# An encoder block on one core: eight attention steps moved into an earlier projection unit, and their operands into a free weight buffer

## The chip, the core and the metric

The kernel runs on one core of a Trainium2 chip. A core has a matrix engine (TensorE, PE in the profile, with its weight loads as PEld), a vector engine (VectorE, DVE), an activation engine (ScalarE, ACT), a general engine (GpSimd, POOL) and a queue that issues transfers (SyncE, SP). Each engine works through its own list of instructions in order, and a semaphore makes one wait for another. Matmuls write into PSUM, which is used here as eight banks of 128 x 2 KB; a bank can take a new result only once the last reader of the old one is through.

The metric is the device time of one execution in microseconds (us): the median of 3 runs of the kernel before is 972.11 us (970.75 to 972.4).

## The reference, cut to what matters

One encoder layer over two sequences with 16 meta tokens each; the 18 blocks of 128 tokens are numbered 0 to 17 (2 of the prompt, 16 of the sample).

```python
h = rmsnorm(z)
q, k, v, g_att, c_val, c_glu, g_conv = split(h @ w_in)
q, k = rmsnorm per head of 64            # 8 query heads, 2 key heads
att = windowed_gqa(q, k, v, sink) * silu(g_att)      # keys within 128 tokens, 16 meta keys, a sink logit
u = c_val * sigmoid(c_glu)
y = depthwise conv of width 31 over u, + conv_b
cnv = silu(layernorm(y)) * silu(g_conv)
out = z + concat(att, cnv) @ w_out
```

Everything is float32. A matmul operand is split into a high and a low part and each product is made of three matmuls (high x high, high x low, low x high), which is why the names xh/xl, mch/mcl and ph/pl come in pairs.

## The kernel before

The tokens are handled in two chunks of 9 blocks. Within a chunk the columns of `w_in` are worked through in units of 256 columns: four units of convolution value and gate, two of the convolution's outer gate, two of the attention gate, one of k and v (KV), and two of q. A unit of k, v or q makes one product per block, called `pj`: 24 matmuls of 128x256. The units of the second chunk that matter here are KV (`kv_group`, all nine blocks), q's first half (`keys[-2]`) and q's second half (`keys[-1]`).

Beside the projections three things run.

- The convolution's taps, on DVE, one instruction per tap (L859).
- The layer norm of a block's convolution output, in three steps (`ln_block`, L176 and on). `lnt`: four transposes on PE into one bank (L186), statistics on DVE, reciprocal root on POOL. `zn`: normalisation on DVE (L199). `lnu`: four transposes back on PE into another bank (L205), four Silu on ACT (L208), store.
- What follows each `pj`: for q, squares on ACT (`sqq`), a sum on DVE (`ssq`), a reciprocal root on POOL (`rqq`), and the scaling that reads the bank for the last time, on DVE (`qs`, L913), then a store. For k, the scaled block is transposed on PE (`kt`, L951) and read by ACT and DVE (`ks`).

After the projections come the attention steps ("slots", `slot_step`): scores `S` on PE, bias and row maximum on DVE (`sb`, L378), exponentials on ACT, normalisation on POOL (L413), transposes `pT` on PE (L436), the split into `ph` (ACT) and `pl` (DVE, L448), the products `O` with v on PE (L471), their merge into the gated output (`tmp` on ACT, `at` on DVE, L503) and the output projection `y` on PE (L547). Parts of `w_out` are loaded as `woraw` and split into two halves, a cast on ACT (L293) and a difference on DVE (`wo`, L296).

Fourteen slots (`EARLY`) are started early, between the nine `pj` of q's second half. `spread` (L597) is called after each of them and issues the slots, the splits of `w_out` (from its third call on) and the loads.

The order of instructions is set in two ways. For most of the program a scheduler arranges every engine's list from its own estimate of when operands will be there. From `attention_open` on (L228), POOL is kept in the order in which the code is written (`MAN1`); from `attention_rest` on (L615), PE is as well (`MAN2`). The code itself defers steps with `later` and calls them from `tick`; `LN_WAIT` says how many ticks a block's layer norm waits, and `LTAGS` gives each `pj` of the last units its pair of PSUM banks ("a" to "d").

Of the kernel before, what the change touches and what calls it, by code (L numbers as in the profile page):

```python
# [11 lines left out]
F32 = mybir.dt.float32  # L12
F32R = mybir.dt.float32r
# [5 lines left out]
P = 128  # L19
D = 1024  # L20
ND = D // P
# [7 lines left out]
KV = 2  # L29
# [4 lines left out]
UW = 256  # L34
# [11 lines left out]
CACHE = 2  # L46
WST = 9
W0 = 3
LN_WAIT = (9, 2)
LTAGS = "abdcdcdcd"  # L50
MAN1 = {mybir.EngineType.Pool}
MAN2 = {mybir.EngineType.Pool, mybir.EngineType.PE}
QSLOT = 6
# [3 lines left out]
PIN_X = 7  # L57
PIN_W = 2
I2 = 2
QP = 1  # L60

GROUPS = [(0, 400)] + [(400 + 384 * i, 384) for i in range(5)]
CHUNKS = [[0, 1, 2], [3, 4, 5]]
# [13 lines left out]
def hymba_kernel(  # L77
# [60 lines left out]
    def later(k, f):  # L138
        due.setdefault(clock[0] + k, []).append(f)

    def work_left():
        return bool(conv_q[0] or conv_q[1] or ln_q or due)

    def tick(ns):
        credit[0] += LOAD * ns
        if ln_q and ln_q[0][0]():
# [15 lines left out]

    xp = ctx.enter_context(tc.tile_pool(name="xp", bufs=3, side="left"))
    left_pools = ExitStack()
    right_pools = ExitStack()
# [4 lines left out]
    wr = right_pools.enter_context(tc.tile_pool(name="wr", bufs=1, side="right"))  # L170
# [5 lines left out]
    def ln_block(c, b, ready):  # L176
        if c == 0:
            o = P * b if b < NB_P else 286 + P * (b - NB_P)
        else:
            o = P * (b - 8)  # L180
        st = {}

        def s1():
            pt = psum.tile([P, 512], F32, tag="c" if phase[0] == 1 else "b", name=f"lnt{b}")
            for j in range(NJ):
                nc.tensor.transpose(pt[:, P * j : P * j + P], yt[c, j][:, o : o + P], ident)  # L186
            bs = yp.tile([P, 6], F32, tag="bs", name=f"bs{b}")
            mv = yp.tile([P, 3], F32, tag="mv", name=f"mv{b}")
            nc.vector.bn_stats(out=bs, in_=pt)
            nc.vector.bn_aggr(out=mv[:, 0:2], in_=bs)  # L190
            rsqrt(mv[:, 1:2], mv[:, 1:2], 1.0, LN_EPS)
            nc.gpsimd.tensor_scalar(mv[:, 2:3], mv[:, 0:1], mv[:, 1:2], -1.0, op0=ALU.mult, op1=ALU.mult)
            st["pt"], st["mv"] = pt, mv
            later(1, s2)

        def s2():
            st["zn"] = yp.tile([P, 512], F32, tag="zn", name=f"zn{b}", bufs=3)
            mv = st["mv"]
            nc.vector.tensor_scalar(st["zn"], st["pt"], mv[:, 1:2], mv[:, 2:3], op0=ALU.mult, op1=ALU.add)  # L199
            later(1, s3)  # L200

        def s3():
            pt = psum.tile([P, 512], F32, tag="d" if phase[0] == 1 else "b", name=f"lnu{b}")
# [16 lines left out]
    def attention_open():  # L220

        phase[0] = 2
        y_pools.close()
        man = ExitStack()
        cst['man'] = man
        man.enter_context(tc.manual_schedule(engines=MAN1))
        ap = att_pools.enter_context(tc.tile_pool(name="ap", bufs=2, side="right", reuse_waits="tile"))
        pool["a"] = ap  # L228
        pool["b"] = att_pools.enter_context(tc.tile_pool(name="bp", bufs=2, side="left", reuse_waits="tile"))
        cst["bias"] = bias = ap.tile([P, KV, 4, SW], BF16, tag="bias", name="bias", bufs=1)  # L230
        load_q(0)
        for i in range(2):
            kw.append(ap.tile([P, 2, KV, 400], F32R, tag=f"kw{i}", name=f"kw{i}", bufs=1))
        load_k(0)
        nc.sync.dma_start(bias, bias_c)
        for t in kw:
            nc.gpsimd.tensor_copy(t[:, :, :, P : P + NM], km)
        for i in range(3):
            t = ap.tile([P, 4, 400], F32, tag=f"sb{i}", name=f"sb{i}", bufs=1)
            for n in range(4):  # L240
                if n > 0:
                    nc.gpsimd.memset(t[:, n, 0 : QB * n], 0.0)
                if n < 3:
                    nc.gpsimd.memset(t[:, n, QB * n + SW : 400], 0.0)
            sbs.append(t)
        load_raw(0)
        load_raw(1)
        load_v(0)
        load_v(1)

    def has_left(b):
        return b not in (0, NB_P)
# [22 lines left out]
    def load_raw(n):  # L275

        for nh in range(2):
            raw = wraws[n, nh] = pool["a"].tile([P, 512], F32, tag="woraw", name=f"woraw{n}_{nh}", bufs=4)
            tc.keep_in_program_order(nc.sync.dma_start(raw, w_out[OUT_ORDER[n]][:, 512 * nh : 512 * nh + 512]))

    def split_wo(n):

        e = OUT_ORDER[n]
        for hl in range(2):
            idx = 2 * n + hl
            if idx % 3 == 0:
                slot = idx // 3
                wo_slot[slot] = xp.tile([P, ND, 400], F32R, tag=("xh", "xl")[slot % 2], name=f"wo{slot}")
            flat = wo_slot[idx // 3].rearrange("p a n -> p (a n)")
            wo[e, hl] = flat[:, D * (idx % 3) : D * (idx % 3) + D]  # L290
        for nh in range(2):
            hi, lo = (wo[e, hl][:, 512 * nh : 512 * nh + 512] for hl in range(2))
            tc.keep_in_program_order(nc.scalar.copy(hi, wraws[n, nh]))  # L293

            def low(nh=nh, hi=hi, lo=lo):
                tc.keep_in_program_order(nc.vector.tensor_tensor(lo, wraws[n, nh], hi, op=ALU.subtract))  # L296
                if nh == 1 and n + 2 < 8:
                    load_raw(n + 2)

            later(1, low)  # L300

# [127 lines left out]
    def bank(b, k, kv):  # L429
# [8 lines left out]
        def split():  # L438
            if k == "m":
# [13 lines left out]

    def spread_meta(b, ph):

        pd = pool["a"].tile([P, KV, 4, P], F32R, tag="pd", name=f"pd{b}", bufs=1)
        for kv in range(KV):
            nc.gpsimd.tensor_tensor(
                pd[:, kv],
# [31 lines left out]
    def merge(b, kv):  # L491
# [22 lines left out]
            nc.vector.tensor_tensor(ml[:, pr, :], at[:, pr, :], mh[:, pr, :], op=ALU.subtract)  # L514

        later(2, fin)

    def rest_part(i):
        return cst["rest"][:, i].rearrange("p (j n) -> p j n", n=P)
# [75 lines left out]

    def spread(b):

        spread_n[0] += 1
        if spread_n[0] == QP:
            q_prep(0)  # L600
        upto = EARLY * max(0, spread_n[0] - QP) // (9 - QP)
        while len(slots) > len_all - upto:
            slot_step(*slots.pop(0))
        if 3 <= spread_n[0] <= 8:
            split_wo(spread_n[0] - 3)
        if spread_n[0] == 4:
            load_mix(0)
        if spread_n[0] == 5:
            load_ga(0)

    len_all = len(slots)

    def attention_rest():
        while ln_q:
            tick(0)  # L615
        for _ in range(2):
            tick(0)
        cst["man"].close()
# [1 line left out]
        rest = wl.tile([P, ND, 2, UW], F32R, tag="ws", name="rest")  # L620
        cst["rest"] = rest.rearrange("p a b n -> p (a b n)").rearrange("p (i n) -> p i n", n=512)
        for n in (6, 7):
            later(n - 5, lambda n=n: split_wo(n))
# [4 lines left out]
        att_pools.close()  # L628
        left_pools.close()

    if True:
# [294 lines left out]
        def kv_block(ws, g, o, rows, b):  # L926
# [134 lines left out]
            prep_at[base] = prep_at.get(base, []) + [(0, preps[3 + n3], "scale")]  # L1061

        for i, (c, u, g) in enumerate(items):
            if (c, u) == keys[-1] and g == CHUNKS[c][0]:
                while conv_q[0] or conv_q[1]:
                    tick(3000)
                for _ in range(3):
                    tick(0)
                right_pools.close()
                attention_open()  # L1070
            if u in U_C and g == CHUNKS[c][0]:
                u_tiles(c, u)
            ws = wsplit[c, u]
# [9 lines left out]
            if u in U_C:  # L1083
                c_group(c, u, ws, g)
            elif u in U_Q:
                q_group(ws, u - U_Q[0], g, spread if (c, u) == keys[-1] else lambda b: None)
            elif u == U_KV:
                kv_group(ws, g)
            elif u in U_GC:
# [93 lines left out]
```

## Time and profile before

| | |
|---|---|
| median of 3 runs | 972.11 us |
| the profiled execution: device time | 970.96 us |
| its span (first to last instruction) | 968.7 us |
| TensorE busy | 943.9 us, 97% of the span |
| DVE / ACT / POOL busy | 755.3 / 422.0 / 339.6 us |
| mean granted TensorE clock | 0.996 of full speed |

The profile page gives busy shares over the whole span. It also cuts the span in 40 slices; apart from the first and the last, the slice from 605 to 630 us is the only one in which TensorE is busy less than 90%, and it is the only one in which its granted clock is lower. The windows view gives the busy time of each engine in any stretch, and the timeline the instructions one by one with the idle time ahead of them and what ended it. The device time is 2.3 us longer than the span, which is what lies around the first and last instruction.

### The profile page before, as it was taken

The numbers are of one execution on the slowest core, as the hardware profiler recorded it, in microseconds if no ns is written. First come the engines' busy times: TensorE is split into PE (matmuls) and PEld (weight loads), VectorE is DVE, ScalarE is ACT, GpSimd is POOL, SyncE is SP. The second block draws the span as 40 slices with busy tenths as digits, with TensorE's granted clock in tenths as the row PEclk, the third lists the DMA queues.
The fourth block names the chain that finished last, engine by engine and source line by source line (L and its number), as shares of the span: only waits on it lengthen the run. The fifth ranks groups of instructions, "written<-read, shape, count | busy, mean of one in ns | idle before, by whom it ended". The sixth has DMA issues, their size and how long they took to land.

```text
span 968.7 us, 16209 instructions
## 1 busy us (share of the span) xinstructions
PE 943.9 (97%) x5721; PEld 883.8 (91%) x5721; DVE 755.3 (78%) x1261; ACT 422.0 (44%) x1156; POOL 339.6 (35%) x542
## 2 busy tenths in 40 slices
PE   5999999999999999999999999799999999999998
PEld 4999999999999999999999998678888888888886
DVE  4659999998987699999993565967777677767773
ACT  6621111343467710111112455755666666656661
POOL 5600000364458300000001463755445444445442
PEclk9999999999999999999999999899999999999999
DMA  9653345785735122233335639654555345544422
GB/s 331 224 191 111 131 171 180 265 285 189 229 118 182 66 92 87 88 122 134 136 136 163 212 110 317 193 170 132 162 167 160 126 161 160 170 135 128 139 77 76
DMA packets 112673, 155.72 MB, mean 161 GB/s; under 512 B 9393, under 2 KB 76097, under 8 KB 112593
## 3 DMA queue, kind: packets, MB, share of 16 engines
q1 hardware_dynamic: 112592, 154.69, 47.9%
q8 instruction: 45, 0.74, 0.3%
q14 instruction: 36, 0.29, 0.1%
HBM read 100.35 MB, written 54.31 MB: 160 GB/s over the span
## 4 chain that ended last, share of the span: by engine, by line
PE 93%; DVE 3%; DMA 1%; ACT 1%; issue 1%; POOL 0%; SPq 0%; DVEq 0%; POOLq 0%; ACTq 0%
PE pj L776 42%; PE y L547 20%; PE pj L792 14%; PE O L471 5%; PE pT L436 4%; PE S L323 4%; DMA wraw<-in_w_in 1%; PE O L323 1%; PE lnu L205 1%; PE lnt L186 1%; PE qT L323 1%; DVE wo L296 1%; ACT xh L707 0%; PE pT_m L433 0%; PE kt L951 0%
## 5 line engine op out<-in xcount | busy, mean ns | idle before, releaser
L776 PE MATMUL pj<-xh,ws 128*128 128x384 f32 (+1 forms) x1536 | 397.7, 339 | 2.8 <-ACT xh L707 2.8
L859 DVE SCALAR_TENSOR_TENSOR y<-us,cw,y 128x1167 f32<-128x1167 f32 x240 | 328.9, 1424 | 0.6
L776 PEld LDWEIGHTS pj<-xh,ws 128*128 128x128 f32 x1536 | 281.4, 189 | 3.1 <-ACT xh L707 3.1
L776 PE MATMUL pj<-xl,ws 128*128 128x384 f32 (+1 forms) x768 | 261.2, 340 | 0.0
L547 PE MATMUL y<-wo,rest 128*128 128x512 f32 x648 | 173.3, 404 | 0.0
L792 PE MATMUL pj<-ws,xh 128*128 128x256 f32 (+1 forms) x880 | 163.8, 284 | 2.1 <-DVE qs L913 2.1
L776 PEld LDWEIGHTS pj<-xl,ws 128*128 128x128 f32 x768 | 144.7, 188 | 0.4 <-DVE xl L716 0.3
L792 PEld LDWEIGHTS pj<-ws,xh 128*128 128x128 f32 (+1 forms) x880 | 135.8, 186 | 3.4 <-ACT es L399 1.6
L547 PEld LDWEIGHTS y<-wo,rest 128*128 128x128 f32 x648 | 115.2, 189 | 20.4
L792 PE MATMUL pj<-ws,xl 128*128 128x256 f32 (+1 forms) x440 | 124.0, 282 | 0.0
L390 ACT ACTIVATE sb<-sb,nm 128x304 f32<-128x304 f32 (+4 forms) x144 | 77.1, 535 | 62.4 <-DVE nm L378 60.0
L448 DVE TENSOR_TENSOR pl<-pT,ph 128x512 fp32r<-128x512 f32 x100 | 68.5, 685 | 31.3 <-ACT ph L447 30.5
L884 ACT ACTIVATE go<-pj 128x384 f32<-128x384 f32 x48 | 23.5, 490 | 153.6 <-PE pj L776 144.7
L378 DVE CUSTOM_DVE_ANT_0 sb<-S,bias,vec 128x304 f32<-128x304 f32 (+4 forms) x144 | 73.2, 511 | 13.7 <-PE S L323 10.6
L792 PEld LDWEIGHTS pj<-ws,xl 128*128 128x128 f32 (+1 forms) x440 | 82.2, 187 | 0.2
L124 POOL TENSOR_SCALAR ssk<-ssk 128x2 f32<-128x2 f32 x18 | 6.6, 364 | 210.9 <-ACT sqk L898 210.8
L413 POOL TENSOR_SCALAR sb<-sb,es 128x304 f32<-128x304 f32 (+4 forms) x144 | 74.2, 533 | 3.5
L447 ACT CAST ph<-pT 128x512 fp32r<-128x512 f32 x100 | 58.0, 580 | 31.7 <-PE pT L436 30.8
L124 POOL TENSOR_SCALAR ssq<-ssq 128x4 f32<-128x4 f32 (+2 forms) x55 | 26.8, 487 | 109.5 <-ACT xn L645 77.1
L436 PE MATMUL pT<-ident,sb 128*128 128x128 f32 x400 | 61.0, 273 | 2.6 <-DVE phm L442 2.1
L323 PEld LDWEIGHTS S<-kw,q 128*128 128x128 f32 x288 | 52.8, 188 | 11.6 <-DVE nm L378 0.4
L323 PE MATMUL S<-kw,q 128*128 128x304 f32 (+4 forms) x288 | 62.0, 298 | 0.0
(118 smaller groups left out, 1277.5 us busy)
## 6 DMA issues: line engine op xcount, KB each, us to landing
wd<-ws SPq DMA_DIRECT2D x36, 512.0 KB, 5.5
ws<-wd SPq DMA_DIRECT2D x36, 512.0 KB, 5.8
wraw<-in_w_in SPq DMA_DIRECT2D x52, 256.0 KB, 5.6
xn<-in_z SPq DMA_DIRECT2D x18, 512.0 KB, 5.9
gd<-go SPq DMA_DIRECT2D x48, 192.0 KB, 2.0
yo<-in_z SPq DMA_DIRECT2D x36, 256.0 KB, 3.3
out_y<-yo SPq DMA_DIRECT2D x36, 256.0 KB, 2.4
kw<-kd SPq DMA_DIRECT2D x16, 512.0 KB, 5.2
```

Source lines behind the costliest of these rows:

```text
L323: r = f(*a, **k)
L378: nc.vector.tensor_tensor_reduce(out=sb[:, n, c0:c1], in0=ps[:, 0:w], in1=cst["bias"][:, kv, n, c0 - QB * n : c1 - QB * n], scale=1.0, sca ...
L390: nc.scalar.activation(sb[:, n, c0:c1], sb[:, n, c0:c1], AF.Exp, bias=nm[:, n : n + 1], scale=-1.0, accum_out=rs[:, n : n + 1],)
L413: nc.gpsimd.tensor_scalar(sb[:, k, a0:a1], sb[:, k, a0:a1], es[:, k : k + 1], 1.0, op0=ALU.mult, op1=ALU.mult)
L436: nc.tensor.transpose(pt[:, hl, :], sbt[b, kv][:, hl, KCOL[k] : KCOL[k] + P], ident)
L447: nc.scalar.copy(ph, pt)
L448: nc.vector.tensor_tensor(pl, pt, ph, op=ALU.subtract)
L471: nc.tensor.matmul(o, lhs, t, start=(start and i == 0), stop=(stop and i == 1))
L547: nc.tensor.matmul(ps, mh[mi][:, e % 4, :], wo[e, wi][:, cols], start=(e == 4 and k == 0), stop=(e == 3 and k == 2),)
L776: nc.tensor.matmul(ps[:, :n], ws[:, d, wi, P * half_i : P * half_i + P], x[xi][:, d, o : o + n], start=(k == 0), stop=(k == 3 * ND - 1),)
L792: nc.tensor.matmul(ps[:rows, :UW], x[xi][:, d, o : o + rows], ws[:, d, wi, :], start=(k == 0), stop=(k == 3 * ND - 1),)
L859: nc.vector.scalar_tensor_tensor(y[:, yo + o0 : yo + o1], u[:, o0 + k : o1 + k], cw[:, j, k : k + 1], y[:, yo + o0 : yo + o1], op0=ALU.mul ...
```

## The change

`attention_open`, which opens the buffers of the scores and clears them, moves from the start of q's second half to the first call of `spread` in q's first half; `spread` now runs after all 18 `pj` of q. Of the 14 early slots, 8 (`EARLY1`) are spread over the calls 4 to 9, and 6 over the second half. To free the space, the pool `right_pools` is closed there, while the convolution's tiles (`y_pools`) stay open until `mixing_open` at call 9.

The operands of the products with v (`ph`, `pl`, `pd`) no longer have buffers of their own in the score pool. They are parts of `ptiles`, a tile in a weight buffer that is free by then. `woraw` has 3 buffers instead of 4 and is loaded one part at a time, the load of part i+3 behind the difference of part i; the splits of `w_out` come at calls 12 to 17.

The layer norm waits one tick instead of two in the second chunk, and the banks are shared out anew: `lnt` takes pair "c" (banks 0 and 1), `lnu` and `kt` take pair "d" (banks 6 and 7), and `LTAGS` is longer, so that q's first half uses pairs "d" and "b" for its `pj`.

```diff
-LN_WAIT = (9, 2)
-LTAGS = "abdcdcdcd"
+LN_WAIT = (9, 1)
+LTAGS = "dbdbdbdb" + "dcdcdcdcd"
-QP = 1
+QP = 3
+EARLY1 = 8
...
     def attention_open():
         phase[0] = 2
-        y_pools.close()
+        right_pools.close()
...
-        load_raw(0)
-        load_raw(1)
         load_v(0)
         load_v(1)
+
+    def mixing_open():
+        while ln_q:
+            tick(0)
+        flush(3)
+        y_pools.close()
+        pool["b"] = att_pools.enter_context(tc.tile_pool(name="bp", bufs=2, side="left", reuse_waits="tile"))
+        pt = wr.tile([P, ND, 2, UW], F32R, tag="ws", name="ptiles")
+        cst["pt"] = pt.rearrange("p a b n -> p (a b n)").rearrange("p (i n) -> p i n", n=512)
+        for i in range(3):
+            load_raw(i)
...
-                if nh == 1 and n + 2 < 8:
-                    load_raw(n + 2)
+                if 2 * n + nh + 3 < 16:
+                    load_raw(2 * n + nh + 3)
...
-            ph = pool["a"].tile([P, 4, P], F32R, tag="ph", name=f"ph{b}_{k}_{kv}", bufs=3)
-            pl = pool["a"].tile([P, 4, P], F32R, tag="pl", name=f"pl{b}_{k}_{kv}", bufs=3)
+            ph, pl = (pt_part(2 * (n_bank[0] % 3) + i) for i in range(2))
+            n_bank[0] += 1
...
     def spread(b):
-        spread_n[0] += 1
-        if spread_n[0] == QP:
+        n = spread_n[0] = spread_n[0] + 1
+        if n == 1:
+            flush(4)
+            attention_open()
+        if n == QP:
             q_prep(0)
-        upto = EARLY * max(0, spread_n[0] - QP) // (9 - QP)
+        if n == 9:
+            mixing_open()
+        if n == 11:
+            load_mix(0)
+        if n == 12:
+            load_ga(0)
+        upto = EARLY1 * max(0, n - QP) // (9 - QP) if n <= 9 else EARLY1 + (EARLY - EARLY1) * (n - 9) // 9
         while len(slots) > len_all - upto:
             slot_step(*slots.pop(0))
-        if 3 <= spread_n[0] <= 8:
-            split_wo(spread_n[0] - 3)
+        if 12 <= n <= 17:
+            split_wo(n - 12)
...
-                pt = psum.tile([P, 512], F32, tag="c", name=f"kt{b}")
+                pt = psum.tile([P, 512], F32, tag="d", name=f"kt{b}")
```

Since the scheduler and the pools decide the order, three places of the program are shown as the engines will work through them.

TensorE at the last layer norms, before: the transposes of one block stand inside the projections of q's first half.

```order
L792 MATMUL pj_5905<-ws_6_4966,xh_3414 128x256 x2
L205 MATMUL lnu_5788<-ident,zn_5740 128x128 x4
L186 MATMUL lnt_5833<-ident,y_0_3683 128x128
L186 MATMUL lnt_5833<-ident,y_1_3869 128x128
L186 MATMUL lnt_5833<-ident,y_2_4172 128x128
L186 MATMUL lnt_5833<-ident,y_3_4550 128x128
L792 MATMUL pj_5905<-ws_6_4966,xl_3415 128x256
```

The same engine now, between the second and the third `pj` of q's first half (`pj_5728` ends just ahead of `lnu_5473` and `kt_5536`, which precede the first row with `lnt_5591`):

```order
L215 MATMUL lnu_5542<-ident,zn_5483 128x128 x4
L979 MATMUL kt_5606<-ident,kn_5520 128x128 x2
L196 MATMUL lnt_5712<-ident,y_0_3683 128x128
L196 MATMUL lnt_5712<-ident,y_1_3869 128x128
L196 MATMUL lnt_5712<-ident,y_2_4172 128x128
L196 MATMUL lnt_5712<-ident,y_3_4550 128x128
L215 MATMUL lnu_5612<-ident,zn_5552 128x128 x4
L215 MATMUL lnu_5627<-ident,zn_5623 128x128 x4
L820 MATMUL pj_5680<-ws_6_4966,xh_2966 128x256
L820 MATMUL pj_5680<-ws_6_4966,xl_2967 128x256
```

Four `lnu`, two `lnt` and two `kt` stand in a row with no projection among them. `lnu_5404`, `lnu_5473`, `lnu_5542`, `lnu_5612` and then `pj_5680` lie in bank 6; both `kt` and `lnu_5627` in bank 7.

TensorE where q's last projection meets the first products with v, before (the last `pj` are through):

```order
L471 MATMUL O_1_6525<-ph_1_1_6485,v_5993 128x512
L471 MATMUL O_1_6525<-pl_1_1_6486,v_5993 128x512
L323 MATMUL O_0_6402<-pd_6482,vm 128x512
L547 MATMUL y_0_6583<-wo_6136,mch 128x512 x2
L323 MATMUL O_1_6525<-pd_6482,vm 128x512
L471 MATMUL O_1_6525<-ph_2_1_6561,v_5995 128x512
```

And now; `pj_6514` (24 matmuls) and a pair of scores stand ahead of these rows, and `pj_6446` is the last projection:

```order
L490 MATMUL O_1_6429<-ptiles,v_5676 128x512 x2
L342 MATMUL O_0_6210<-ptiles,vm 128x512
L342 MATMUL O_1_6429<-ptiles,vm 128x512
L490 MATMUL O_1_6429<-ptiles,v_5678 128x512 x2
L820 MATMUL pj_6446<-ws_7_5554,xh_3414 128x256
```

A whole projection now stands behind the products, in bank 1, which `O_0_6210` held until its merge has read it. Behind its 24 matmuls come `y_0_6572` x6, `S_1_2`, `qT_6582`, `y_0_6572` x6, `S_1_3`, `pT_0_0`, and then `y_1_6633`, which lies in bank 6, the bank of `pj_6514`.

DVE ahead of the last `qs` of q, before (`qs_17` is the last reader of `pj_6492`):

```order
L296 TENSOR_TENSOR wo_6411<-woraw_0_6308,wo_6318 128x512
L913 TENSOR_TENSOR qs_16_6455<-pj_6414,rqq_16_6443 128x256
L296 TENSOR_TENSOR wo_6411<-woraw_1_6310,wo_6318 128x512
L296 TENSOR_TENSOR wo_6411<-woraw_0_6358,wo_6411 128x512
L448 TENSOR_TENSOR pl_2_1_6562<-pT_2_1_6543,ph_2_1_6561 128x512
L296 TENSOR_TENSOR wo_6411<-woraw_1_6360,wo_6411 128x512
L530 TENSOR_TENSOR mcl<-cn_6199,mch 128x512
L503 TENSOR_TENSOR at_6599<-O_0_6402,tmp_0_6600 64x256 x2
L913 TENSOR_TENSOR qs_17_6537<-pj_6492,rqq_17_6521 128x256
```

And now; ahead of these rows stand `ssq_16`, `ssq_17` and two `wo`:

```order
L533 TENSOR_TENSOR rest<-at_6588,rest 128x256 x2
L397 ISA sb_5655,nm_1_6502<-S_1_2_6579,bias,vec 128x208
L397 ISA nm_1_6502 128x1
L315 TENSOR_TENSOR wo_6594<-woraw_0_6489,wo_6594 128x512
L554 TENSOR_TENSOR rest<-cn_6495,rest 128x512
L941 TENSOR_TENSOR qs_16_6491<-pj_6446,rqq_16_6475 128x256
L364 TENSOR_TENSOR q_2_6587<-qT_6582,q_2_6587 64x4x4x32
L365 TENSOR_TENSOR q_2_6587<-qT_6582,q_2_6587 64x4x4x32
L397 ISA sb_5655,nm_1_6502<-S_1_3_6608,bias,vec 128x176
L397 ISA nm_1_6502 128x1
L467 TENSOR_TENSOR ptiles<-pT_0_0_6628,ptiles 128x512
L941 TENSOR_TENSOR qs_17_6556<-pj_6514,rqq_17_6543 128x256
```

The merges (`at`) now stand ahead of the stretch, and the split of the third query block (`q_2`) and the score step `S_1_3` stand in it.

## Rows read from the trace of the kernel before

**Rows 1.** The page: the chain of work that ended last, shares by engine.

```profile
PE 93%; DVE 3%; DMA 1%; ACT 1%; issue 1%; POOL 0%; SPq 0%; DVEq 0%; POOLq 0%; ACTq 0%
```

**Rows 2.** Windows: length, busy PE, PEld, DVE, ACT, POOL, granted clock, DMA.

```profile
600.00:640.00 40.00, 32.51 (x180) 25.91 (x181) 34.57 (x90) 27.56 (x76) 25.67 (x36) 0.91 0.61 189
```

**Rows 3.** Windows of 2 us from 590 to 640, and their sum.

```profile
600.00:602.00 2.00, 1.20 (x10) 1.23 (x11) 2.00 (x8) 1.98 (x7) 0.00 (x0) 1.00 1.04 345
...
612.00:614.00 2.00, 0.17 (x2) 0.00 (x0) 1.97 (x8) 2.00 (x7) 0.39 (x2) 1.00 0.88 274
614.00:616.00 2.00, 0.91 (x4) 0.51 (x4) 1.97 (x3) 1.43 (x4) 2.00 (x2) 0.63 0.58 205
616.00:618.00 2.00, 0.92 (x2) 0.83 (x3) 2.00 (x4) 1.38 (x3) 2.00 (x3) 0.50 0.16 49
...
620.00:622.00 2.00, 1.59 (x5) 0.85 (x5) 1.99 (x5) 0.62 (x1) 1.56 (x2) 0.66 0.91 271
...
sum 50.00, PE 41.65 PEld 34.57 DVE 42.11 ACT 34.31 POOL 30.46; mean PE 1.67 PEld 1.38 DVE 1.68 ACT 1.37 POOL 1.22
```

**Rows 4.** Timeline of TensorE: start, duration, instruction, idle before it and its releaser.

```profile
600.80 0.36 PE L792 MATMUL pj<-ws,xh 128*128 128x256 f32 x1 [1.40 <-DVE qs L913]
...
614.27 0.91 PE L436 MATMUL pT<-ident,sb 128*128 128x128 f32 x4 [2.11 <-DVE phm L442]
617.08 0.77 PE L471 MATMUL O<-ph,v 128*128 128x512 f32 x1 [1.90 <-DVE qs L913]
...
632.44 0.33 PE L433 MATMUL pT_m<-ident,pm 128*128 128x128 f32 x1 [1.04 <-POOL pm L404]
632.52 1.63 PE L547 MATMUL y<-wo,rest 128*128 128x512 f32 x6
633.99 0.39 PE L323 MATMUL S<-kw,q 128*128 128x240 f32 x2
```

**Rows 5.** Timeline of DVE in the same stretch.

```profile
613.03 0.73 DVE L894 TENSOR_REDUCE ssq<-sqq 128x4 f32<-128x256 f32 x2
...
616.86 2.64 DVE L296 TENSOR_TENSOR wo<-woraw,wo 128x512 fp32r<-128x512 f32 x2
...
622.09 0.42 DVE L913 TENSOR_TENSOR qs<-pj,rqq 128x256 f32<-128x256 f32 x1
622.79 0.85 DVE L503 TENSOR_TENSOR at<-O,tmp 64x256 f32<-64x256 f32 x2 [0.27 <-ACT tmp L501]
```

**Rows 6.** Timeline of TensorE at one layer norm.

```profile
541.75 0.60 PE L186 MATMUL lnt<-ident,y 128*128 128x128 f32 x4
542.19 0.38 PE L951 MATMUL kt<-ident,kn 128*128 128x128 f32 x2
542.41 0.60 PE L205 MATMUL lnu<-ident,zn 128*128 128x128 f32 x4
```

**Rows 7.** Timeline of DVE at the same layer norm.

```profile
545.01 0.81 DVE L199 TENSOR_SCALAR zn<-lnt,mv 128x512 f32<-128x512 f32 x1 [1.32 <-POOL mv L192]
```

**Rows 8.** Timeline of ACT: the Silu of a layer norm.

```profile
543.05 1.50 ACT L208 ACTIVATE zn<-lnu,vec 128x128 f32<-128x128 f32 x4
```

**Rows 9.** Lines, 575 to 640 us: count, busy us, mean ns, idle before.

```profile
L296 DVE TENSOR_TENSOR wo<-woraw,wo 128x512 fp32r<-128x512 f32 x16 | 13.6, 873 | 0.0
...
L378 DVE CUSTOM_DVE_ANT_0 sb<-S,bias,vec 128x176 f32<-128x176 f32 (+3 forms) x21 | 8.9, 442 | 1.7 <-PE S L323 1.5
...
L448 DVE TENSOR_TENSOR pl<-pT,ph 128x512 fp32r<-128x512 f32 x8 | 5.5, 684 | 1.8 <-ACT ph L447 1.7
...
L893 ACT ACTIVATE sqq<-pj 128x256 f32<-128x256 f32 x10 | 3.6, 382 | 4.4 <-PE pj L792 4.2 <-DVE ssq L894 0.2
...
L345 DVE TENSOR_TENSOR q<-qT,q 64x512 fp32r<-64x512 f32 x3 | 2.0, 683 | 9.5 <-ACT q L344 9.5
...
L501 ACT COPY tmp<-O 64x512 f32<-64x512 f32 x3 | 1.8, 584 | 2.1 <-PE O L323 1.9 <-DVE at L503 0.2
```

**Rows 10.** Timeline of POOL at q's last blocks.

```profile
616.01 2.94 POOL L458 TENSOR_TENSOR pd<-phm,vec 128x512 fp32r<-128x512 f32 x2
```

More of the change, by code (lines that the diff above doesn't have):

```diff
@@ L142, in work_left, with flush @@
         return bool(conv_q[0] or conv_q[1] or ln_q or due)
+    flushing = [False]
+    def flush(n):
+        flushing[0] = True
+        for _ in range(n):
+            tick(0)
+        flushing[0] = False
     def tick(ns):
         credit[0] += LOAD * ns
-        if ln_q and ln_q[0][0]():
+        if ln_q and not flushing[0] and ln_q[0][0]():
             ln_q.pop(0)[1]()
@@ L164, in hymba_kernel @@
     left_pools = ExitStack()
+    wr_pools = ExitStack()
     right_pools = ExitStack()
@@ L169, in hymba_kernel @@
     yp = y_pools.enter_context(tc.tile_pool(name="yp", bufs=4, side="left"))
-    wr = right_pools.enter_context(tc.tile_pool(name="wr", bufs=1, side="right"))
+    wr = wr_pools.enter_context(tc.tile_pool(name="wr", bufs=1, side="right"))
     sp = right_pools.enter_context(tc.tile_pool(name="sp", bufs=2, side="right"))
@@ L183, in s1 @@
         def s1():
-            pt = psum.tile([P, 512], F32, tag="c" if phase[0] == 1 else "b", name=f"lnt{b}")
+            pt = psum.tile([P, 512], F32, tag="c", name=f"lnt{b}")
             for j in range(NJ):
@@ L202, in s3 @@
         def s3():
-            pt = psum.tile([P, 512], F32, tag="d" if phase[0] == 1 else "b", name=f"lnu{b}")
+            pt = psum.tile([P, 512], F32, tag="d" if phase[0] == 1 else "c", name=f"lnu{b}")
             for j in range(NJ):
@@ L228, in attention_open @@
         pool["a"] = ap
-        pool["b"] = att_pools.enter_context(tc.tile_pool(name="bp", bufs=2, side="left", reuse_waits="tile"))
         cst["bias"] = bias = ap.tile([P, KV, 4, SW], BF16, tag="bias", name="bias", bufs=1)
@@ L245, in attention_open @@
             sbs.append(t)
-        load_raw(0)
-        load_raw(1)
         load_v(0)
         load_v(1)
+    def mixing_open():
+        while ln_q:
+            tick(0)
+        flush(3)
[5 more added lines that the diff above has]
+            load_raw(i)
     def has_left(b):
@@ L273, in load_q, with load_raw @@
         nc.sync.dma_start(qt[b].rearrange("p a e -> p (a e)"), qd[b])
[L275 to L279, printed above, removed]
+    def load_raw(i):
+        n, nh = divmod(i, 2)
+        raw = wraws[n, nh] = pool["b"].tile([P, 512], F32, tag="woraw", name=f"woraw{n}_{nh}", bufs=3)
+        tc.keep_in_program_order(nc.sync.dma_start(raw, w_out[OUT_ORDER[n]][:, 512 * nh : 512 * nh + 512]))
     def split_wo(n):
@@ L454, in spread_meta @@
     def spread_meta(b, ph):
-        pd = pool["a"].tile([P, KV, 4, P], F32R, tag="pd", name=f"pd{b}", bufs=1)
+        pd = cst["pt"][:, 6:8].rearrange("p a (j n) -> p a j n", n=P)
         for kv in range(KV):
@@ L516, in merge, with pt_part @@
         later(2, fin)
+    n_bank = [0]
+    def pt_part(i):
+        return cst["pt"][:, i].rearrange("p (j n) -> p j n", n=P)
     def rest_part(i):
@@ L596, in spread @@
     def spread(b):
-        spread_n[0] += 1
-        if spread_n[0] == QP:
-            q_prep(0)
-        upto = EARLY * max(0, spread_n[0] - QP) // (9 - QP)
+        n = spread_n[0] = spread_n[0] + 1
[3 more added lines that the diff above has]
+        if n == QP:
+            q_prep(0)
+        if n == 9:
[5 more added lines that the diff above has]
+        upto = EARLY1 * max(0, n - QP) // (9 - QP) if n <= 9 else EARLY1 + (EARLY - EARLY1) * (n - 9) // 9
         while len(slots) > len_all - upto:
             slot_step(*slots.pop(0))
-        if 3 <= spread_n[0] <= 8:
-            split_wo(spread_n[0] - 3)
[L606 to L609, printed above, removed]
+        if 12 <= n <= 17:
+            split_wo(n - 12)
     len_all = len(slots)
     def attention_rest():
-        while ln_q:
-            tick(0)
         for _ in range(2):
@@ L622, in attention_rest @@
         for n in (6, 7):
-            later(n - 5, lambda n=n: split_wo(n))
+            later(2 * n - 11, lambda n=n: split_wo(n))
         while slots and (todo or slots[0][0] < NB):
@@ L628, in attention_rest @@
         att_pools.close()
+        wr_pools.close()
         left_pools.close()
@@ L1063, in hymba_kernel @@
         for i, (c, u, g) in enumerate(items):
-            if (c, u) == keys[-1] and g == CHUNKS[c][0]:
+            if (c, u) == keys[-3] and g == CHUNKS[c][0]:
                 while conv_q[0] or conv_q[1]:
                     tick(3000)
[L1067 to L1070, printed above, removed]
             if u in U_C and g == CHUNKS[c][0]:
@@ L1085, in hymba_kernel @@
             elif u in U_Q:
-                q_group(ws, u - U_Q[0], g, spread if (c, u) == keys[-1] else lambda b: None)
+                q_group(ws, u - U_Q[0], g, spread if (c, u) in keys[-2:] else lambda b: None)
             elif u == U_KV:
```

## The prediction

> **What bounds the kernel now.** I read the chain of waits on the page first: 93% of the span is TensorE's own work [rows 1]. A change that leaves the matmuls alone can gain only where TensorE stands idle or runs at a lower clock. The windows view was next: from 600 to 640 us TensorE is busy for 32.51 of 40 us, at a mean granted clock of 0.91 [rows 2]. That is the end of q's second half, the place the change is about. Cut in pieces of 2 us, the stretch from 590 to 640 has TensorE busy for 41.65 of 50 us, so 8.35 us are idle [rows 3]. DVE is busy nearly all the time in the rows shown.
>
> The timeline then tells what ends the idle time: 2.11 us until DVE's `phm`, 1.90 us until DVE's `qs`, later 1.04 us until POOL's `pm` [rows 4]. Behind the first two, the granted clock is 0.50 of full speed, 1.2 of 2.4 GHz, in the window from 616 us, and 0.63 and 0.66 in those from 614 and 620 us [rows 3]. Four transposes that are worth 0.44 us at full speed (from `lnt` to the next start, [rows 6]) take 0.91 us [rows 4]. From 617.08 to about 621 us work of half that length is done at half speed, so the clock costs some 2.0 + 0.2 = 2.2 us. All that this place can give back is 8.35 + 2.2 = 10.5 us.
>
> **The change part by part.** It adds and removes no matmul. I work against the profiled execution: 970.96 us, span 968.7, so 2.3 us around it. The median of the runs is 972.11, so 1.15 us are added at the end.
>
> *What goes.* Eight of the fourteen slots leave the stretch with their scores and two splits of q. A score takes DVE 0.44 us, a split two halves of 0.68 [rows 9]; they find DVE with room in q's first half. The last `qs` came at 622.09 us [rows 5], long after its projection. I take the 8.35 us and the 2.2 us of clock as gone, and look for what is late next. Three things are.
>
> *The layer norms.* With a shorter wait they are denser, and all `lnu` but two lie in bank 6. Between `pj_5728` and `pj_5680` the list has no projection to cover them. An `lnu` may be written only when the Silu of the one before is through, and `pj_5680` needs the Silu of the third. From `lnu` to Silu is 0.64 us (542.41 to 543.05 [rows 6, 8]) and the Silu is 1.50 us [rows 8]: 3 x 2.14 = 6.4 us, or 7.2 if ACT's two `ks`, which stand between them, don't fit in the gaps. TensorE has 4 `lnu` and 2 `lnt` of 0.44 us and 2 `kt` of 0.22 us [rows 6] to do, 3.1 us. It waits 3.3 to 4.1 us; I take 3.7. The bottom is 3 x 1.94 - 3.1 = 2.7 us, without any hand-over, and it can't be below that, since the bank is one. The top is 6, if a `zn` is late too: from `lnt` to the end of `zn` is 4.07 us (541.75 to 545.82 [rows 6, 7]), and `lnt_5591` starts only behind `lnu_5473`, so that a slip on DVE or POOL of 2 us shows. In before this place had none of that.
>
> *The last projection.* `pj_6446` waits for the merge of `O_0_6210`: `tmp` on ACT, 0.58 us [rows 9], and a pair of `at` on DVE, 0.85 us [rows 5], with hand-overs 1.6 us, less the three products of `O_1` that stand between (each a sixth of the 1.47 us that six matmuls of that width take from start to start [rows 4], 0.7 us together): 0.9 us at least. ACT and DVE each have a part of `w_out` ahead of the merge, worth up to 0.87 us [rows 9], and the products themselves wait for `pd`, 2.94 us a pair on POOL [rows 10]. I take 1.7, between 0.9 and 4.
>
> *The last `qs`.* `y_1_6633` lies in the bank of `pj_6514` and waits for `qs_17`. DVE can start on this stretch with the squares of `pj_6446`, 0.38 us [rows 9] and two hand-overs after its end, say 0.7 us. Up to and with `qs_17` it has: two `ssq` (0.73), three `wo` (3 x 0.87), `rest` twice as a pair of `at` (0.85), `rest` of the convolution as a `pl` (0.68), two scores (0.88), two `qs` (0.84), a split of q (1.36) and a `pl` (0.68) [rows 5, 9], together 8.6 us. Neighbours overlap by some 0.07 us and most `wo` are quicker than their mean, so I take 7.5. TensorE has 2 x 1.47 of `y` and about 1.1 us of scores and transposes in that time, 4.0 us. Wait: 0.7 + 7.5 - 4.0 = 4.2 us, 3.5 to 6 (two `wo` took 2.64 us once, beside POOL's `pd` [rows 5, 10]). Queued behind `y_1` on TensorE are all scores of the next block, so nothing else can go ahead. The lower end would come only if DVE found its parts of `w_out` always there.
>
> *What stays and what moves free.* Of the waits of before behind 622 us, I leave 1.0 us (0 to 2.5): the one for `pm` has the same order on POOL now. The loads and clears of `attention_open` come earlier, beside the last KV and q projections, where neither POOL nor the queue has TensorE waiting; the `woraw` loads, one by one in three buffers, are covered by the `qs` and scores between the `wo`; without that cover they lengthen the last wait, which its top end holds. The parts of `ptiles` cost nothing by themselves: three pairs as before. At the end of the first chunk some transposes and the scaling of the next x move up on TensorE and DVE; what they need is there, and the DVE time is the same, so I count zero there.
>
> *The clock.* Two pauses, 4.0 us in 4.9, preceded the fall in before, while a single one of 1.40 us, ended at 600.80 us [rows 4], left it at 1.00 [rows 3]. The wait for `qs_17` is as long as the two together: I take one fall there, 2.2 us (0 to 2.2).
>
> The Trainium skill, "TensorE: Matmul & The Clock Gate", section "A second HAM failure mode: psum-queue depth-cycling", says that a TensorE that pauses briefly and often between groups while PSUM banks cycle loses its full clock again and again. The layer norm place would be such a case, four short groups on one bank; by the rule the sum rises by the price of one fall. The pauses around 600 us, which were fewer, don't show it.
>
> Sum: 3.7 + 1.7 + 4.2 + 1.0 + 2.2 = 12.8 us lost in place of 10.5: +2.3 us, 973.2 on the profiled execution's scale and 974.4 on the median's.
>
> **The rivals.**
>
> *The relief wins.* The three waits come out at their lower ends (2.7 + 0.9 + 3.5), nothing stays behind them, and the clock holds: 7.1 against 10.5, 968.7 us. For it: DVE loses 6.2 us of work here (8 scores of 0.44, two splits of 1.36), and its queue is what ended the long pauses. Against it: the waits that I found are of one bank or one merge, and DVE's lead doesn't shorten them. If also the layer norms' wait hides, it is 966.
>
> *The clock falls at the layer norms too.* TensorE does 3.1 us of work in seven, in pieces of 0.44 to 1 us, and the clock falls as it did behind 614 us: a further 2.2 us, 976.6, and 979 if the waits are together 2.4 us longer as well. For it: the same share of idle time as in the two pauses before. Against it: no single pause is much longer than the 1.4 us that left the clock alone.
>
> *The time only moves.* The idle time and the one fall of before are found again, spread over two places, in the same amount: 972 us. For it: the same work on DVE ends the stretch.
>
> **How the numbers follow.** The forecast has 0.40, with a range of its own of 972.5 to 976. The relief has 0.27, the second fall 0.18, no change 0.15. A measurement of this kernel can tell about 0.2%, 1.9 us, from no change. Faster by more than that: the relief and little else, 0.28. Slower: most of the forecast (from 974.05, so 0.26) and the second fall, 0.44. Within: 0.28. The range of 966.5 to 979 leaves out what lies beyond the relief with the layer norms hidden and beyond two falls with the waits at their tops, 2 in 10.
>
> **What would show it.** Right: TensorE idle for 3 to 4 us between the second and third projection of q's first half, released by ACT's Silu; 1 to 2 us ahead of the last projection, released by DVE's `at`; some 4 us ahead of the first `y_1`, released by DVE's `qs`; a granted clock of 0.50 behind the last of these alone; the idle time from 590 to 615 us nearly gone. A stretch of q's second half without a pause over 1 us would make the forecast wrong, and so would a layer norm place in which the `lnu` follow each other without waiting.

## The result, and the profile after

The changed kernel takes 976.15 us (median of 7 runs, 974.28 to 978.65), the kernel before 971.92 us beside it. The ratio is 1.0048, with a 95% interval of 1.0034 to 1.0063: slower by 4.2 us, where the prediction had 2.3. The profiled execution took 975.67 us, with a span of 973.7, 5.0 us more than before.

Windows of the kernel after, with the columns of [rows 2]:

```profile
550.00:600.00 50.00, 44.56 (x362) 43.45 (x361) 24.66 (x67) 26.17 (x71) 23.63 (x63) 0.97 0.74 238
600.00:640.00 40.00, 33.42 (x214) 29.60 (x212) 27.78 (x66) 20.86 (x52) 21.52 (x30) 0.91 0.56 169
```

From 600 to 640 us TensorE is idle for 6.58 us, against 7.49 in [rows 2]; the pauses between 600 and 612 us are gone and others stand behind them. From 550 to 600 us 5.44 us are idle. In before that was 0.86 (the rest of the 8.35 us of [rows 3]). So the loss lies at the layer norms, some 50 us ahead of the place that the eight steps were taken from.

TensorE's timeline after has these waits (start, duration, instruction, idle before it and its releaser), those from 557 us at the layer norms, those from 615 us at the end of q's second half:

```profile
557.95 1.11 PE L196 MATMUL lnt<-ident,y 128*128 128x128 f32 x4 [3.86 <-DVE zn L209]
...
561.51 0.66 PE L215 MATMUL lnu<-ident,zn 128*128 128x128 f32 x4 [0.32 <-ACT zn L218]
563.38 0.63 PE L215 MATMUL lnu<-ident,zn 128*128 128x128 f32 x4 [1.21 <-DVE zn L209]
...
615.82 0.70 PE L490 MATMUL O<-ptiles,v 128*128 128x512 f32 x2 [1.51 <-DVE qs L941]
...
619.10 0.35 PE L820 MATMUL pj<-ws,xh 128*128 128x256 f32 x1 [1.65 <-DVE at L522]
...
627.14 1.57 PE L455 MATMUL pT<-ident,sb 128*128 128x128 f32 x4 [1.34 <-POOL sb L432]
630.54 1.19 PE L571 MATMUL y<-wo,mch 128*128 128x512 f32 x2 [1.82 <-DVE es L421]
```

They answer to [rows 4] and [rows 6]. At the layer norms 5.39 us are lost in three pauses, at the end 6.32 us in four. The last one's releaser, `es`, follows the last `qs`, which starts at 629.98 us; DVE had it in front. The first pause, of 3.86 us at 557.95 us, is the one that the prediction didn't have, and the chain that ended last says what is behind it (start, duration, what):

```profile
548.27 8.79 DMA cd<-zn
...
557.08 0.82 DVE zn L209
...
557.95 1.11 PE lnt L196 x4
```

A layer norm's result goes from `zn` to memory (`cd`) and the buffer comes free when the store has landed; there are three such buffers. This store took 8.79 us. `lnt` can't go on meanwhile, since its bank is read by the `zn` that waits. SP's timeline shows what was issued just ahead of it: the four parts of 512 KB of the weights for q's second half.

```profile
545.73 1.84 SPq L761 DMA_DIRECT2D ws<-wd  x4
...
548.27 0.56 SPq L221 DMA_DIRECT2D cd<-zn  x1
```

DVE, in order, stood still for 3.65 us with the next `zn`:

```profile
557.08 0.81 DVE L209 TENSOR_SCALAR zn<-lnt,mv 128x512 f32<-128x512 f32 x1 [3.65 <-DMA cd<-zn]
```

ACT waited in the same way with the next `ks`, for a buffer that the store of an earlier `ks`, issued right behind, still held:

```profile
557.83 0.47 ACT L986 ACTIVATE ks<-kt,kscale 128x256 fp32r<-128x256 f32 x1 [2.42 <-DMA kd<-ks]
```

Before had the same weights load at 543.29 us, a `zn` store among its parts that took 6.9 us, and nobody who waited for it. The difference is how close the layer norms stand. In before their `lnu` are spread over the projections, on TensorE's timeline:

```profile
553.35 0.60 PE L205 MATMUL lnu<-ident,zn 128*128 128x128 f32 x4
...
558.13 0.60 PE L205 MATMUL lnu<-ident,zn 128*128 128x128 f32 x4
...
563.38 0.60 PE L205 MATMUL lnu<-ident,zn 128*128 128x128 f32 x4
```

The granted clock, which in before fell once [rows 3], falls twice. TensorE's windows of after (length, busy PE, granted clock, DMA share, GB/s):

```profile
558.00:560.00 2.00, 2.00 (x10) 0.50 0.07 23
560.00:562.00 2.00, 1.69 (x10) 0.72 0.46 131
```

and at the end, with all engines' columns:

```profile
630.00:632.00 2.00, 1.46 (x4) 1.20 (x5) 0.64 (x4) 0.00 (x0) 1.09 (x3) 0.50 1.00 333
632.00:634.00 2.00, 2.00 (x8) 1.71 (x7) 0.00 (x0) 0.62 (x1) 1.04 (x3) 0.50 1.03 388
634.00:636.00 2.00, 2.00 (x8) 1.71 (x7) 2.00 (x4) 1.72 (x3) 0.00 (x0) 0.50 0.13 44
```

What a fall costs can be worked out from such windows of 2 us: busy time times one minus the granted clock, summed up. The table gives idle time and clock cost of TensorE in two stretches of every profiled execution, this way. What is left of a span without these four numbers lies between 955.7 and 958.9 us. Each row is one execution, and the mean granted clock is not the same in all executions of a kernel, nor is the time: after has 0.991 in three of seven (977.01 to 978.65 us), 0.995 in the profiled one and 0.996 in the fastest (974.28 us); e7 has 0.996 in four of ten, the profiled one among them (969.83 to 970.73 us), and 0.993 in six (970.92 to 972.61 us); e72 has 0.996 in all five.

| kernel | median, us | ratio to before, 95% | idle, clock 546–576 | idle, clock 600–650 | span |
|---|---|---|---|---|---|
| before | 971.92 | | 0.0, 0.0 | 7.5, 2.3 | 968.7 |
| after | 976.15 | 1.0034–1.0063 | 5.4, 1.5 | 6.6, 3.0 | 973.7 |
| Silu out of `zn` (e1) | 975.84 | 1.0028–1.0054 | 3.5, 2.8 | 6.9, 1.6 | 973.0 |
| weights later (e2) | 974.57 | 1.0021–1.0040 | 2.9, 1.6 | 7.1, 4.3 | 973.8 |
| four `woraw` (e5) | 976.01 | 1.0028–1.0053 | 5.1, 1.4 | 6.9, 3.8 | 974.2 |
| `EARLY` 12 (e6) | 976.10 | 1.0025–1.0054 | 4.9, 1.4 | 5.3, 3.0 | 972.2 |
| no step early (e8) | 975.19 | 1.0019–1.0043 | 5.1, 2.7 | 4.3, 4.9 | 974.8 |
| layer norms wait two groups (e9) | 974.34 | 1.0019–1.0037 | 3.5, 1.4 | 6.3, 6.0 | 973.5 |
| banks apart (e7) | 971.27 | 0.9984–1.0003 | 1.3, 0.0 | 6.8, 3.2 | 968.2 |
| e7 and `EARLY` 12 and e2 (e726) | 970.25 | 0.9974–0.9993 | 2.0, 0.0 | 5.8, 3.0 | 968.4 |
| e7 and e2 and e9 (e729) | 969.83 | 0.9970–0.9989 | 1.1, 0.0 | 7.1, 2.4 | 966.3 |
| **e7 and e2 (e72)** | **969.12** | 0.9957–0.9983 | 2.0, 0.0 | 5.5, 2.7 | 966.3 |

### The profile page after: what moved, and what is told of

Read it like the earlier page. It is cut to its first block, busy times and chain, and to the rows that moved or that the text cites. A ratio compares the mean times of both kernels' runs of the same rounds, so it can differ in the third digit from the quotient of the medians.

```text
span 973.7 us, 16190 instructions
## 1 busy us (share of the span) xinstructions
PE 945.0 (97%) x5721; PEld 886.8 (91%) x5721; DVE 755.3 (78%) x1261; ACT 421.9 (43%) x1156; POOL 343.1 (35%) x542
## 4 chain that ended last, share of the span: by engine, by line
PE 93%; DMA 2%; DVE 2%; ACT 1%; POOL 1%; issue 1%; SPq 0%; POOLq 0%; ACTq 0%
PE pj L804 42%; PE y L571 20%; PE pj L820 14%; PE O L490 5%; PE pT L455 4%; PE S L342 4%; DMA cd<-zn 1%; PE O L342 1%; PE qT L342 1%; PE lnt L196 1%; DMA woraw<-in_w_out 1%; PE lnu L215 1%; DMA xn<-in_z 1%; PE pT_m L452 0%; ACT zn L218 0%
## 5 line engine op out<-in xcount | busy, mean ns | idle before, releaser
L467 DVE TENSOR_TENSOR ptiles<-pT,ptiles 128x512 fp32r<-128x512 f32 x100 | 68.6, 686 | 31.6 <-ACT ptiles L466 30.9
L466 ACT CAST ptiles<-pT 128x512 fp32r<-128x512 f32 x100 | 58.0, 580 | 35.8 <-PE pT L455 35.0
L490 PE MATMUL O<-ptiles,v 128*128 128x512 f32 x200 | 64.3, 402 | 1.5 <-DVE qs L941 1.5
```

The costliest lines, as they stand in the source:

```text
L490: nc.tensor.matmul(o, lhs, t, start=(start and i == 0), stop=(stop and i == 1))
```

## The experiments

Four theories stood against each other. A: the layer norms wait for `zn` buffers that a slow store holds. B: they wait for one another's bank, as predicted. C: the end waits for the loads of `woraw`, which are issued one by one in three buffers. D: the end is set by the order of the merges and normalisations on DVE and POOL, whichever load or score comes first.

**e1, the buffer freed early.** The Silu of the second chunk writes into the convolution's tile, no longer needed, and the store reads from there, as four stores of 64 KB in place of one of 256 KB (the stores' lines are left out here).

```diff
+            dst = [yt[c, j][:, o : o + P] if c else cn[:, j, :] for j in range(NJ)]
-                    cn[:, j, :], pt[:, P * j : P * j + P], AF.Silu, ...
+                    dst[j], pt[:, P * j : P * j + P], AF.Silu, ...
```

> Changed kernel, but in the second chunk the Silu of a layer norm writes into the convolution tile that it came from, and the store reads that tile (four stores of 64 KB instead of one of 256 KB), so that a zn buffer is free as soon as TensorE has read it. Theory A (the 3.86 us pause at 554 us is the third zn buffer, held by a store that took 8.79 us): the pause goes, what stays there is the chain of Silu in bank 6, 3.3 us or less in place of 5.4 us, the clock may hold; 976.15 falls to 972 to 974. Theory B (my prediction: the bank chain alone ends the wait): idle time there stays at 5 us or more, 976.

975.84 us, no gain that can be measured over after; neither answer came out whole, since the idle time fell to 3.5 us and the time didn't follow. No `zn` waits for a store any more. TensorE's waits at the layer norms of e1:

```profile
556.83 0.66 PE L215 MATMUL lnu<-ident,zn 128*128 128x128 f32 x4 [0.94 <-ACT y L219]
557.86 0.44 PE L988 MATMUL kt<-ident,kn 128*128 128x128 f32 x2 [0.37 <-DVE ks L996]
559.08 0.66 PE L215 MATMUL lnu<-ident,zn 128*128 128x128 f32 x4 [0.79 <-ACT y L219]
561.09 1.12 PE L215 MATMUL lnu<-ident,zn 128*128 128x128 f32 x4 [1.35 <-DVE ks L996]
```

The four come to 3.45 us. Two, 1.73 us together, end on the Silu (`y` here): that is the bank chain. The other two end on `ks`, the last reader of the other bank, and the longest goes back to a store once more, that of an earlier `ks` (there are two buffers):

```profile
560.04 0.47 ACT L995 ACTIVATE ks<-kt,kscale 128x256 fp32r<-128x256 f32 x1 [1.01 <-DMA kd<-ks]
```

That store went out at 557.03 us, 2.6 us after its `ks` was through: SP was busy issuing four of the smaller stores, so e1's own edit has a part in this pause. The total is like the predicted 3.3 to 4.1 us, but the banks are shown for some 2 us of it only. And the clock falls without any pause over 1.35 us:

```profile
560.00:562.00 2.00, 0.91 (x5) 0.50 0.66 183
...
564.00:566.00 2.00, 2.00 (x12) 0.50 0.50 139
```

**e2, the weights sent later.** The last weights load goes out behind the stores of the second chunk's layer norms.

```diff
...
+                        put = lambda part=part, q=q: eng.dma_start(part.bitcast(F32), wd[key[1], q])
+                        if key == keys[-1]:
+                            later(9 + q, lambda put=put: tc.keep_in_program_order(put()))
+                        else:
+                            put()
...
```

> Changed kernel, but the 2 MB of weights for q's second half are loaded behind the stores of the layer norms instead of ahead of three of them; the order on TensorE at the layer norms is the same to a few rows. Theory A: the stores land in 2 to 3 us instead of up to 8.79, the pause of 3.86 us goes, 972 to 974, as in the run beside it. Theory B: no change, 976. If the weights now come too late, a new wait for them ahead of the first projection of q's second half shows, and the time is above 976.

974.57 us, some 1.7 us better than after by the ratios (1.0030 against 1.0048), with intervals that overlap. From 543 to 561 us the stores of `zn` land in 2.0 to 3.0 us, as theory A had it, but the time stays above its 972 to 974. (The longest store, 7.1 us, is that of a later block, behind parts of the weights; nothing at these layer norms waits for it.) Five pauses of 0.46 to 0.76 us remain, 2.90 us in all, ended by `zn`, `ks` and the Silu, and the clock still goes to 0.50. With the slow store cured, theory B's waits are left.

**e5, a fourth `woraw` buffer**, for theory C.

```diff
-        for i in range(3):
+        for i in range(4):
             load_raw(i)
...
-        raw = ... tag="woraw", ..., bufs=3)
+        raw = ... tag="woraw", ..., bufs=4)
...
-                if 2 * n + nh + 3 < 16:
-                    load_raw(2 * n + nh + 3)
+                if 2 * n + nh + 4 < 16:
+                    load_raw(2 * n + nh + 4)
```

> Changed kernel with four buffers for the parts of w_out in place of three (loads four ahead). Theory C (the pauses of 3.2 us around 615 us come from loads of w_out, one by one in three buffers: ACT waited 9.4 us for them): these pauses shrink by 1 to 2 us, 974 to 975. Rival D (the merge of the first products, which stands ahead of the last projection, sets it): the waits for the loads shrink and the time stays at 976 within 1 us.

976.01 us. C falls: from 590 to 640 us ACT waits 5.0 us for these loads in place of 9.4, and the end's idle time is 6.9 us, where after has 6.6. The projection ahead of the merge now waits longer, for the same `at`:

```profile
618.42 0.48 PE L820 MATMUL pj<-ws,xh 128*128 128x256 f32 x1 [2.43 <-DVE at L522]
```

**e6, two slots fewer in the second half.**

```diff
-EARLY = 14
+EARLY = 12
```

> Changed kernel with 12 early attention steps in place of 14 (8 in q's first half as before, 4 in the second), so that the products with the meta keys and the merge stand behind the last projection on TensorE. Rival D: the 3.2 us around 615 us go, and a part comes back in front of the first output projections; 973 to 975. Theory C: the loads of w_out still come late and the idle time of the stretch stays 6.6 us or so; 976.

976.10 us. The idle time at the end falls by 1.3 us in the profiled execution, and the median doesn't move, so neither theory gains by it. Other waits come in their place, the largest for POOL:

```profile
618.50 0.49 PE L342 MATMUL S<-kw,q 128*128 128x240 f32 x2 [1.42 <-DVE nm L397]
620.56 0.79 PE L342 MATMUL O<-ptiles,vm 128*128 128x512 f32 x1 [1.57 <-POOL ptiles L477]
```

**e7, the banks apart.** Two products of q's first half, among which the layer norms stand, no longer use the pair in which `lnu` lies, so that the scheduler may put a projection between two `lnu`.

```diff
-LTAGS = "dbdbdbdb" + "dcdcdcdcd"
+LTAGS = "ababdbdb" + "dcdcdcdcd"
```

> Changed kernel with other banks for the second to fifth projection of q's first half (pairs a and b in place of d and b), so that no projection has to wait for the Silu in bank 6 and the scheduler puts projections between the layer norms' transposes. Theory B (one bank for all lnu and then a projection: the chain that was still there, 3.5 us idle, when the zn buffers were free early): the idle time at 554 to 564 us falls below 2 us, the clock stays at 1.00 there, 970.5 to 973. Theory A alone (the store that holds a zn buffer): the wait of some 3.5 us stays, 974 to 976.

971.27 us, level with before (0.9984 to 1.0003) and 5 us under after: the largest effect of one edit. In the profiled execution the `lnu` stand apart again with projections between them, one pause is left, and the clock holds there (timeline and windows of e7):

```profile
558.63 0.60 PE L215 MATMUL lnu<-ident,zn 128*128 128x128 f32 x4
...
560.93 0.60 PE L215 MATMUL lnu<-ident,zn 128*128 128x128 f32 x4
...
562.78 0.66 PE L215 MATMUL lnu<-ident,zn 128*128 128x128 f32 x4 [1.26 <-DVE ks L987]
```

```profile
560.00:562.00 2.00, 1.53 (x14) 1.00 0.66 202
562.00:564.00 2.00, 1.22 (x11) 1.00 0.20 69
```

The store is as slow as in after (up to 8.7 us), and DVE still waits for it, 2.25 us ahead of one `zn`:

```profile
556.44 0.81 DVE L209 TENSOR_SCALAR zn<-lnt,mv 128x512 f32<-128x512 f32 x1 [2.25 <-DMA cd<-zn]
```

But TensorE has projections to do meanwhile. So the store of A held TensorE up in after because the list, which B's banks had left without projections, gave it no cover.

**e72, e7 and e2 together** (no new lines).

> Both cures of the layer norm place: the banks of the run beside it, and the weights of q's second half loaded behind the stores. If both waits were in series (A and B, one behind the other), nothing is left there: idle below 0.5 us from 545 to 600, no fall of the clock before 600 us, 970 to 972. If one of them is enough, the same time as the run beside it.

969.12 us, ratio 0.9970 with 0.9957 to 0.9983: faster than before, and the lowest median, though the intervals of e726 and e729 overlap with it. It is lower than expected, and not because nothing is left at the layer norms: their idle time is 2.0 us, more than in e7. The clocks given above the table tell what differs from e7: in none of the five executions did the mean fall below 0.996, while in six of e7's ten it did, which its profiled execution doesn't show. So the place of the load still counts with the banks apart, where the two intervals just don't meet; where e7's clock falls in those six is not known. Against before, its span is 2.4 us shorter; the stretches of the table, with the 0.86 us of before between 576 and 600 us, hold 0.5 of that, the first 30 us another 0.5 (18.91 us busy against 18.45), and the rest was not located. The idle time at the end is 5.5 us; the projection's wait for the merge is shorter than in after, and the last one is the same:

```profile
612.08 0.36 PE L827 MATMUL pj<-ws,xh 128*128 128x256 f32 x1 [0.96 <-DVE at L525]
...
623.45 1.19 PE L574 MATMUL y<-wo,mch 128*128 128x512 f32 x2 [1.83 <-DVE es L424]
```

**e726, e72 with `EARLY` 12.**

> As the run with banks and late weights, with 12 early steps in place of 14, so that the last projection isn't behind the merge. If the waits around 615 us cost by themselves: 1 to 2 us below that run, 968.5 to 971. If DVE's and POOL's work for the last blocks ends the stretch anyway: the same time within 1 us.

970.25 us: no gain at the end here either, where the sum of idle time and clock is 8.7 us, against 8.2 in e72.

**e8, no step early.** The change without its eight moved steps: buffers, pools and order stay.

```diff
-EARLY1 = 8
+EARLY1 = 0
```

> Changed kernel with no attention step in q's first half; all 14 in the second, as before, with buffers, banks and w_out parts as in the changed kernel. If moving the 8 steps is what relieved the end of q's second half: idle time from 590 to 640 us goes up from 6.6 to 8 us or more, 977 to 979. If it bought nothing there: 976 within 1 us.

975.19 us, with an interval that overlaps that of after. Whether the eight steps are moved or not makes no difference that was measured; the layer norms' idle time is about the same (5.1 us), and the end has less idle time (4.3 us) but more at a low clock (4.9). The slower time comes from what the change does around the steps, and e7 shows the part that matters most: the banks.

**e9, the layer norms wait for two groups again.**

```diff
-LN_WAIT = (9, 1)
+LN_WAIT = (9, 2)
```

> Changed kernel with one part undone: the layer norms of the second chunk may start after two groups again, not after one. TensorE's list still has three lnu and two lnt in a row between the second and third projection of q's first half, with two projections more ahead of the last pair. Theory B (the bank chain, with the store of zn in front of it): the zn stores are no longer four in the shadow of the weights load, so the wait of 3.9 us for zn is gone or below 1 us, but three lnu in one bank still wait for two Silu, some 2 us and perhaps the clock's fall: 973 to 975 us. Rival, the wait constant itself is the cause: the layer norm place has under 1 us of pauses and the time is that of the kernel before, 971 to 972. Rival, the place doesn't matter: 976.

974.34 us, inside theory B's 973 to 975, with an interval that just overlaps that of after. Three `lnu` and two `lnt` still stand together in the list, behind the same load. Two waits for `zn` are left at the layer norms, not below 1 us as expected:

```profile
554.95 0.66 PE L196 MATMUL lnt<-ident,y 128*128 128x128 f32 x4 [1.21 <-DVE zn L209]
...
558.25 1.09 PE L215 MATMUL lnu<-ident,zn 128*128 128x128 f32 x4 [2.20 <-DVE zn L209]
```

In its chain a store of 6.94 us stands ahead of the first of them. The wait constant alone is not the cause.

**e729, all three.**

> Changed kernel with the last layer norms alternating between banks, the last weights load sent behind the zn stores, and the wait of two groups: in TensorE's list every lnt and lnu now stands inside or beside a projection. Theory: no pause over 0.5 us and a clock of 1.00 from 550 to 575 us, where the version with two of the three edits had 0.16 + 0.78 + 1.06 us; the end of q's second half as there, 5.5 us of idle time and one fall: 967.5 to 969 us. Rival, the end of the half takes back what the layer norms give (the later layer norms push the keys, the scores and mixing_open back): 969 to 971 us, with more than 6.5 us idle from 600 to 650.

969.83 us, with 7.1 us of idle time from 600 to 650: the rival's answer, and not better than e72. From 550 to 571 us TensorE has no pause any more, so the idle time of the layer norms can be had back there. But the weights now come late once, and the end takes back 1.6 us of idle time:

```profile
571.91 0.35 PE L827 MATMUL pj<-ws,xh 128*128 128x256 f32 x1 [1.11 <-DMA ws<-wd]
...
608.48 0.70 PE L493 MATMUL O<-ptiles,v 128*128 128x512 f32 x2 [1.44 <-DVE qs L948]
612.22 0.36 PE L827 MATMUL pj<-ws,xh 128*128 128x256 f32 x1 [2.12 <-ACT wo L315]
```

Of the theories on the end only D is left, but it is not shown: no edit brought idle time and clock of that stretch under 8 us together. No run changed the order on POOL itself, so which of its steps sets the end stays open.

## Why the prediction was right or wrong

The direction and the three places were right, the size was short by 1.9 us on the medians. On the profiled executions the forecast of +2.3 us stands against +5.0: idle time +3.7 in the stretches of the forecast (12.0 us where 10.6 were forecast, against 8.35 before), busy time +1.1 over the whole span. The clock cost 2.1 us more than in before by the windows; where TensorE is busy 1 us less in return was not located. That the sum came as near as it did is in part luck: the layer norms and the clock were short by 1.7 and 2.2 us, the last `qs` was 2.4 us too long.

- **Layer norms: the term whose path was wrong.** It had 3.7 us, ended by ACT's Silu in bank 6; measured were 5.39, of which 3.86 were ended by a `zn` that waited 3.65 us for the buffer that a store held, 1.21 by the last `zn` behind it, and only 0.32 by a Silu. The bank chain is there (1.73 us behind the Silu in e1), and the banks are what leaves the list without cover (e7), but the prediction followed the bank and not the three `zn` buffers. It put the upper end of 6 down to a slip on DVE or POOL. The queue was named only for the loads of `attention_open`, "where neither POOL nor the queue has TensorE waiting", and the weights load was not counted at all. The cure by banks alone (e7) is worth 5 us by the ratios; by the store alone it is 0.7 (e1) to 1.7 (e2), neither clear of the noise.
- **The clock: the second fall came.** One fall of 2.2 us was in the sum, the second was a rival at 976.6, which is nearest to the 976.15 measured, with the second fall where it said. By the windows the falls cost 1.5 us at the layer norms and 3.0 at the end. The Trainium skill, "TensorE: Matmul & The Clock Gate", section "A second HAM failure mode: psum-queue depth-cycling", would have raised the sum by one fall. In after the fall followed a pause of 3.86 us and doesn't need that rule; in e1, with four pauses of 0.37 to 1.35 us between groups that share banks, the clock fell too, which agrees with it, and with the one pause of 1.26 us in e7's profiled execution it didn't.
- **The last projection** was to wait 1.7 us for the merge; it waited 1.65, for `at`, as worked out.
- **The last `qs`** was to cost 4.2 us ahead of `y_1`; it cost 1.82. DVE's part was right: from the end of `pj_6446` to that of `qs_17` 8.2 us pass, as forecast. What was short is TensorE's own part, 5.2 us where 4.0 were counted, and 1.34 us of the wait come ahead of the transposes `pT`, for POOL's `sb`, which the working didn't have; those four transposes alone took 1.57 us. Another `qs` holds up `O` for 1.51 us, which was not forecast. So the end as a whole, 6.3 us, is close to the 6.9 of the terms (1.7 + 4.2 + 1.0) by errors that cancel.
- **What goes:** the pauses of [rows 4] were taken as gone, and those up to 615 us nearly are (0.70 us idle from 590 us, against 3.79 in before), but others stand behind; from 600 to 650 us idle time and clock are 9.8 us in before, 9.5 in after and 9.2 without the moved steps (e8). The rival "the relief wins" has nothing to rest on.
- **Counted at nothing** was the reorder at the end of the first chunk. From 200 to 400 us TensorE is busy for 198.94 us in before and 198.97 in after, so that was right.

## What to carry to other kernels

Before a group of small steps is packed closer, follow every buffer that the group turns over, its store in memory and what is queued ahead of that store included, and not only the PSUM bank. A wait that another wait covers gives nothing back when it is cured alone: e1, e2 and e9 brought 0.7 to 1.9 us each, by the ratios, hardly more than the noise, while e7, which let projections in between, brought 5. Work that moves off a busy stretch changes what is late there; here the eight steps bought nothing, and the gain that was to be had (3 us under before in e72) lay in the banks of two projections and the place of one load.

## What was not expected of the hardware

- A store of 256 KB that lands in 2.0 us at best took 8.79 us when four loads of 512 KB had been issued 2.5 us ahead on the same queue, and the next two took 6.2 and 4.7 us. In e2 and e72, where those loads go out later, the stores of the same layer norms took 2.0 to 3.0 us.
- The length of a pause alone doesn't tell whether the clock falls. In after 1.51 and 1.65 us of waiting, 615 to 619 us, left it at 1.00, and so did 1.44 and 2.12 us in e729; 0.66 and 2.45 us in e9 were followed by 0.50, and so were the four short ones of e1. The windows of e9 and e729 behind those pauses:

```profile
616.00:618.00 2.00, 1.51 (x7) 0.50 0.73 255
```

```profile
612.00:614.00 2.00, 1.78 (x15) 1.00 0.68 236
```
